# Attention with the queries on partitions: the product with V, the division and the norm by token row

## The chip, the cores and the metric

The kernel runs on one core of one Trainium2 chip. The metric is the device time of one execution in microseconds (us). A core has five engines, each with its own queue of instructions that it works through in order: TensorE (PE, matrix products and transposes, with PEld for its weight loads), VectorE (DVE), ScalarE (ACT), GpSimd (POOL) and SyncE (SP), which here issues the transfers (DMA). An engine that waits for one instruction's operands holds up all that stands behind it in its queue.

## The reference

One step of a decoder layer, for 1024 prompt tokens and 8 running sequences of 8 tokens each (64 sample tokens), width 1024:

```python
x = x + 0.5 * rms_norm(swiglu(rms_norm(x, norm_ffn1_pre), ffn1_w_gu, ffn1_w_down), norm_ffn1_post)
h = rms_norm(x, norm_mix_pre)
z = h @ w_in + b_in
q, k, v, hq, hf, hi, hg = jnp.split(z, cumsum(IN_SPLITS)[:-1], axis=-1)
a, k_new, v_new = attend(q, k, v, attn_sinks)     # 8 heads of 64, 2 kv heads, window 128
a = rms_norm(a, attn_out_norm)                    # over all 512 columns of a token
...                                               # HGRN2 on hq, hf, hi, hg gives o
mix = jnp.concatenate([a, o], axis=-1) @ w_out
x = x + rms_norm(mix, norm_mix_post)
x = x + 0.5 * rms_norm(swiglu(rms_norm(x, norm_ffn2_pre), ffn2_w_gu, ffn2_w_down), norm_ffn2_post)
```

The probabilities of a head divide by a sum that has the sink as one more term:

```python
m = jnp.maximum(jnp.max(s, axis=-1, keepdims=True), sk)
p = jnp.exp(s - m)
den = jnp.sum(p, axis=-1, keepdims=True) + jnp.exp(sk - m)
return p / den
```

For the prompt, attention works in blocks of 128 queries against 256 keys (the block before and its own).

## The kernel before

**Groups and stages.** The tokens are worked on in three groups: group 0 holds two prompt blocks of 128 and the 64 sample tokens (320 columns), groups 1 and 2 hold three prompt blocks each (384). The stages are FFN1, the mixer and FFN2. In the mixer, `w_in_units(n)` makes the projections of group n, `mixer(n)` runs attention and HGRN2 on it, `w_out_units(n)` multiplies with w_out. Every large product is three products in fp32r (`mm` L278, L279, L280: high and low parts), so a weight that arrives by DMA (`raw`, L262 or L880) is split by ACT (L255) and DVE (L256: `w`, `wspl`) before PE can use it.

**What sets the order.** PE should always have large products, and the small work goes between them. Attention blocks (`attn_block`, L1110), HGRN2 blocks (`hgrn_block`), norms and transposes are generators. `mixer(n)` runs one step of HGRN2 and one of attention in turn. Between the units of a large product `tick()` advances these streams by rates (1.0 step for mixer 1 and 1.3 for mixer 2 among them); `need(name)` finishes one that must be done. Each `yield` in a generator ends a step. So the products of FFN1 of group 1 run beside the mixer of group 0, those of `w_in_units(2)` and w_out beside the mixer of group 1, and so on. After that a scheduler orders the instructions once, when the program is built, by buffers that come free and by its own model of durations; the order on each engine is then fixed.

**Buffers.** Tiles of [128, 512] come from a ring of 8 (`t2`): the probabilities, their transposes, rows of x (`xt`), squares and outputs share it. PE writes small results to 4 PSUM banks (`ax`) and products to 4 others (`mm`). `raw` has 3 slots.

**Attention of one block.** For each of two values of pr (two heads of each of the two kv heads): scores (`sc`, L1127), mask and row maximum (L1135), exponent with row sum (L1144), the sink's exponent (L1146, L1147), sum and reciprocal (L1149, L1150), scaling of the probabilities (L1156 on ACT for g = 1, L1158 on DVE for g = 0), 8 transposes into two banks `pT` (L1165), two copies to SBUF on DVE (L1168), and the product with V. There V is stationary (64 columns for one kv head) and the transposed probabilities of two heads move:

```python
PE.matmul(ob[64 * g:64 * g + 64, pr * 256:pr * 256 + 256],
          vn[:, vb, g * 64:g * 64 + 64],
          pT[g][:, :2 * wk].rearrange("p (i k t) -> p k i t", i=2, k=nk)[:, kb], ...)
```

The result `pv` has features on partitions and tokens on columns. `finish_attn_t` (L1087) takes the norm over features: squares on ACT (L1090), four products with a column of ones (`ms`, L1094), reciprocal root on DVE (L241 to L249), a diagonal matrix (L1098), a product of ones with it (L1100) that puts the factor on all partitions, a copy (L1102) and four multiplications on DVE (L1105). `put_mix` (L1064) writes high and low parts for w_out (L1067, L1068). The sample tokens, whose result has tokens on partitions, go through `finish_attn` (L1070).

**The input of group 1 to the mixer.** This stream, "c1", runs beside the end of FFN1 and the mixer of group 0. `half_n` multiplies FFN1's result with a row of gains (`gb`, loaded at L400), `post_n` adds the input x: for three blocks and two halves a tile `xt` is loaded (L424), DVE computes `big` from it (L426), and `x1N` is stored (L427). `pre_n` takes the next norm (L394 and on), and PE transposes the result (`tr`, L454) to `h` (L458, L459), which `w_in_units(1)` multiplies.

**The bias row.** The 512 columns of the HGRN value projection have their bias on the columns: a row tile `bhi` that is loaded once at the start of the mixer and added at L1057.

## Time and profile before

| | |
|---|---|
| time, median of 3 runs | 2049.44 us (2048.64 to 2050.24) |
| span of the profiled execution | 2045.3 us |
| mean granted clock of PE | 0.988 |
| profiled execution's own time | not listed apart; the median is 4.1 us above the span |
| DVE, ACT, POOL busy | 71%, 46%, 27% of the span |

The span runs from the first to the last instruction. A granted clock below 1 means that PE worked at a lower rate for part of the time. The slices of part 2 of the page show how busy each engine is in each fortieth of the span (51 us each); the digits are tenths:

```profile
PE   9999999999999999899999998999999999999998
DVE  5776667885568557777678756766889888655667
PEclk9999999999999999799999998999999999999999
```

The 7 in the third row stands at slice 17, the 8 at slice 25. The mixer lies between about 628 and 1410 us.

### The profile page before, as it was taken

Reading aid. Unit: us, or ns where it says so; the run is one execution under the profiler, and the core shown is the slowest. Engines: PE = TensorE matmul, PEld = TensorE weight load, DVE = VectorE, ACT = ScalarE, POOL = GpSimd, SP = SyncE. Lnnn points to the kernel's source line nnn. Section 1 sums busy time; section 2 is a strip of 40 time slices with the busy share of each in tenths; the row PEclk is TensorE's granted clock in tenths of the full one; section 3 lists DMA queues with packets and bytes.
Section 4 is the critical chain, followed back from the end, with each engine's and each line's share of the span. In section 5 each row is a group of like instructions: output and inputs, shape, how many; then the busy total and the mean of one; then the engine's idle time right before and its main releaser. Section 6 shows DMA issues by size and latency. Waiting matters only on the chain.

```text
span 2045.3 us, 34828 instructions
## 1 busy us (share of the span) xinstructions
PE 2006.7 (98%) x13273; PEld 1856.7 (91%) x13273; DVE 1452.6 (71%) x2493; ACT 933.5 (46%) x1679; POOL 550.1 (27%) x508
## 2 busy tenths in 40 slices
PE   9999999999999999899999998999999999999998
PEld 8999999999998987697898897878999999999886
DVE  5776667885568557777678756766889888655667
ACT  6534333444455445435344444544544444444552
POOL 0013433654113101311113310210046554510201
PEclk9999999999999999799999998999999999999999
DMA  8455445556777545556434243525565556576874
GB/s 254 140 158 169 139 156 164 200 182 219 238 235 213 159 149 171 160 145 184 127 96 138 87 141 94 163 87 184 168 193 200 191 188 209 195 241 222 289 257 136
DMA packets 372368, 360.09 MB, mean 176 GB/s; under 512 B 40590, under 2 KB 294361, under 8 KB 372185
## 3 DMA queue, kind: packets, MB, share of 16 engines
q1 hardware_dynamic: 371401, 356.42, 55.2%
q8 instruction: 104, 1.70, 0.3%
q10 hardware_dynamic: 800, 1.44, 0.2%
q14 instruction: 63, 0.52, 0.1%
HBM read 279.85 MB, written 78.94 MB: 175 GB/s over the span
## 4 chain that ended last, share of the span: by engine, by line
PE 91%; DVE 3%; DMA 3%; ACT 1%; issue 1%; SPq 0%; DVEq 0%; ACTq 0%
PE mm L278 27%; PE mm L279 26%; PE mm L280 26%; PE c L280 1%; PE c L278 1%; PE c L279 1%; PE sc L1127 1%; DMA ar<-fa 1%; PE pv L1176 1%; DMA raw<-in_ffn_w_gu_dram 1%; PE lv L1204 1%; PE pT L1165 1%; PE tr L497 1%; DVE w L256 1%; DMA xt<-in_x_prompt_dram 0%
## 5 line engine op out<-in xcount | busy, mean ns | idle before, releaser
L278 PE MATMUL mm<-h,wsph 128*128 128x320 f32 (+1 forms) x1296 | 414.7, 322 | 3.7 <-ACT sg L632 2.2
L279 PE MATMUL mm<-h,wsph 128*128 128x320 f32 (+1 forms) x1296 | 412.5, 319 | 0.0
L280 PE MATMUL mm<-h,wspl 128*128 128x320 f32 (+1 forms) x1296 | 411.7, 318 | 0.0
L255 ACT CAST wsph<-raw 128x1024 fp32r<-128x1024 f32 x202 | 211.3, 1048 | 293.9 <-PE mm L279 237.1
L256 DVE TENSOR_TENSOR wspl<-raw,wsph 128x1024 fp32r<-128x1024 f32 x202 | 251.0, 1245 | 119.3 <-ACT wsph L255 118.5
L256 DVE TENSOR_TENSOR w<-raw,w 128x512 fp32r<-128x512 f32 (+1 forms) x226 | 250.0, 1110 | 84.9 <-ACT w L255 82.8
L255 ACT CAST w<-raw 128x512 fp32r<-128x512 f32 (+1 forms) x226 | 169.6, 754 | 207.3 <-PE mm L279 109.8
L278 PEld LDWEIGHTS mm<-h,wsph 128*128 128x128 f32 x1296 | 244.6, 189 | 11.0 <-issue 3.1
L280 PEld LDWEIGHTS mm<-h,wspl 128*128 128x128 f32 x1296 | 244.7, 189 | 4.0 <-issue 3.5
L279 PEld LDWEIGHTS mm<-h,wsph 128*128 128x128 f32 x1296 | 245.0, 189 | 3.2 <-issue 2.6
L278 PE MATMUL mm<-h,w 128*128 128x384 f32 x704 | 235.8, 335 | 1.2 <-DVE big L725 1.2
L279 PE MATMUL mm<-h,w 128*128 128x384 f32 x704 | 235.8, 335 | 0.0
L280 PE MATMUL mm<-h,w 128*128 128x384 f32 x704 | 230.5, 335 | 0.0
L279 PE MATMUL mm<-w,h 128*128 128x512 f32 x462 | 181.6, 393 | 0.0
L278 PE MATMUL mm<-w,h 128*128 128x512 f32 x462 | 180.8, 395 | 0.5 <-DVE big L905 0.5
L280 PE MATMUL mm<-w,h 128*128 128x512 f32 x462 | 179.5, 392 | 0.0
L280 PE MATMUL mm<-big,w 128*128 128x384 f32 x528 | 176.8, 335 | 1.5 <-DVE w L256 1.5
L279 PE MATMUL mm<-big,w 128*128 128x384 f32 x528 | 176.7, 335 | 0.0
L278 PE MATMUL mm<-big,w 128*128 128x384 f32 x528 | 176.6, 335 | 0.0
L709 POOL TENSOR_TENSOR big<-big 128x384 f32<-128x384 f32 x88 | 111.7, 1269 | 236.5 <-ACT big L722 116.2
L256 DVE TENSOR_TENSOR w<-t,w 128x512 fp32r<-128x512 f32 x176 | 160.5, 922 | 17.5 <-ACT w L255 17.0
L278 PEld LDWEIGHTS mm<-h,w 128*128 128x128 f32 x704 | 132.2, 188 | 1.6 <-DVE big L725 1.6
(359 smaller groups left out, 3881.2 us busy)
## 6 DMA issues: line engine op xcount, KB each, us to landing
raw<-in_ffn_w_gu_dram SPq DMA_DIRECT2D x156, 512.0 KB
raw<-in_ffn_w_down_dram SPq DMA_DIRECT2D x74, 512.0 KB
raw<-in_w_in_dram SPq DMA_DIRECT2D x54, 512.0 KB
ar<-fa SPq DMA_DIRECT2D x70, 384.0 KB
big<-in_ffn_w_down_dram SPq DMA_DIRECT2D x88, 256.0 KB
fb<-big SPq DMA_DIRECT2D x44, 512.0 KB
raw<-fb SPq DMA_DIRECT2D x40, 512.0 KB
fa<-big SPq DMA_DIRECT2D x22, 768.0 KB
```

Of the source, the lines that this page charges most:

```text
L255: S.copy(hi, src)
L256: (lo_eng or V).tensor_tensor(lo, src, hi.bitcast(F32), op=ALU.subtract)
L278: PE.matmul(out, a[0], b[0], start=first, stop=False, skip_group_check=resume)
L279: PE.matmul(out, a[0], b[1], start=False, stop=False, skip_group_check=resume)
L280: PE.matmul(out, a[1], b[0], start=False, stop=last, skip_group_check=resume)
L497: PE.transpose(bank[:, i * P:(i + 1) * P], y[kh][:, i, k * P:(k + 1) * P], ident)
L709: G.tensor_tensor(e[:, i], e[:, i], e[:, i + 1], op=ALU.mult)
L1127: PE.matmul(banks[g][:, i * 256:i * 256 + wk], zq[64 * g:64 * g + 64, 2 * pr + i, b * P:(b + 1) * P], kx[64 * g:64 * g + 64, k0:k0 + wk], ...
L1165: PE.transpose(bank[:, (i * nk + kb) * P:(i * nk + kb + 1) * P], pt[g][:, i, kb * P:(kb + 1) * P], ident)
L1176: PE.matmul(ob[64 * g:64 * g + 64, pr * 256:pr * 256 + 256], vn[:, vb, g * 64:g * 64 + 64], pT[g][:, :2 * wk].rearrange("p (i k t) -> p k ...
L1204: PE.matmul(b4[cs, a, :32], x[:, a, cs], y[:, a, cs], start=True, stop=True)
```

## The change

For the prompt blocks the roles in the product with V are swapped: the transposed probabilities (128 x 128) are stationary, and the 64 columns of V move. Its result has tokens on partitions and 512 features on columns. The probabilities are not divided before they are transposed. After both values of pr the sink's exponent, the sums and the reciprocals are taken once for 8 heads, and one multiplication of 128 x 512 divides the result. The norm is `finish_attn`, as for the sample tokens: square with a row sum on ACT, one multiplication with the row's factor and the norm weights, which lie as a row tile (`aon`), four transposes (`oT`), and `put_mix` straight from PSUM. `finish_attn_t` is gone. The copy of the second `pT` bank moves from DVE to ACT. `aon` takes the place of `bhi` in its pool; `bhi` is loaded in each `w_in_units` into a tile of the ring of 8. An attention block has 11 steps instead of 10, the samples' finish 3 instead of 2. Lines behind the removed ones have smaller numbers: L426 is now L422, L256 is L252, L278 to L280 are L274 to L276.

```diff
--- before.py
+++ after.py
@@ -158,10 +158,6 @@
         put(C_HGN, A["hg_out_norm"], 1)
-        for half in range(2):
-            nc.sync.dma_start(rows[C_AON:C_AON + 4, half * 64:half * 64 + 64],
-                              A["attn_out_norm"][0:1, half * 256:half * 256 + 256].rearrange(
-                                  "o (m d) -> (o m) d", d=64))
         bank = axbank()
...
@@ -972,8 +968,11 @@
         def t2(shape=(P, 512)):
             return tmp2("t2", shape)
 
-        bhi = tp.tile([P, 512], F32, tag="bhi", name="bhi")
-        nc.sync.dma_start(bhi, A["b_in"][0:1, 1792:2304].partition_broadcast(P))
+        aon = tp.tile([P, 512], F32, tag="aon", name="aon")
+        for half in range(2):
+            nc.sync.dma_start(aon.rearrange("p (m g d) -> p g m d", m=4, g=2)[:, half],
+                              A["attn_out_norm"][0:1, half * 256:half * 256 + 256].partition_broadcast(P).rearrange(
+                                  "p o (m d) -> p (o m) d", d=64))
 
...
@@ -1045,6 +1044,8 @@
             S.activation(z["hq"][:, :, :w], z["hq"][:, :, :w], AF.Silu)
             hv = z["v"] = big(F32, (P, 3, 512))
+            bhi = tmp2("bhi")
+            nc.sync.dma_start(bhi, A["b_in"][0:1, 1792:2304].partition_broadcast(P))
             banks = [mmbank() for _ in range(nb)]
...
@@ -1073,38 +1074,13 @@
             S.activation(junk[:r], o[:r], AF.Square, accum_out=sm[:r, 0, 0:1])
             V.tensor_scalar(sm[:r, 0, 0:1], sm[:r, 0, 0:1], 1.0 / 512, EPS, op0=ALU.mult, op1=ALU.add)
             rsqrt(sm[:r, 1, 0:1], sm[:r, 0, 0:1], (sm[:r, 2, 0:1], sm[:r, 3, 0:1]))
-            V.tensor_scalar(o[:r], o[:r], sm[:r, 1, 0:1], None, op0=ALU.mult)
+            V.scalar_tensor_tensor(o[:r], o[:r], sm[:r, 1, 0:1], aon[:r], op0=ALU.mult, op1=ALU.mult)
+            yield
             yield
             b4 = axbank("oT").rearrange("p (c t) -> p c t", c=4)
             for c in range(4):
                 PE.transpose(b4[:, c, :r], o[:r, c * P:(c + 1) * P], ident[:r, :r])
-            m = t2((P, 4, P))
-            V.tensor_tensor(m[:, :, :r], b4[:, :, :r],
-                            cols[:, C_AON:C_AON + 4].unsqueeze(2).to_broadcast([P, 4, r]), op=ALU.mult)
-            put_mix(n, 0, sl, m[:, :, :r])
-            yield
-
-        def finish_attn_t(n, ob, sl):
-
-            sm, sq = small(), t2()
-            S.activation(sq, ob, AF.Square)
-            yield
-            bank = axbank("ms")
-            for m in range(4):
-                PE.matmul(bank[:, P:P + 1], sq[:, m * P:(m + 1) * P], ones[:, 0:1], start=m == 0, stop=m == 3)
-            V.tensor_scalar(sm[:, 0, 0:1], bank[:, P:P + 1], 1.0 / 512, EPS, op0=ALU.mult, op1=ALU.add)
-            rsqrt(sm[:, 1, 0:1], sm[:, 0, 0:1], (sm[:, 2, 0:1], sm[:, 3, 0:1]))
-            dg = sq[:, :P]
-            V.tensor_scalar(dg, ident, sm[:, 1, 0:1], None, op0=ALU.mult)
-            yield
-            PE.matmul(bank[:, :P], ones, dg, start=True, stop=True)
-            rb = sq[:, P:2 * P]
-            S.copy(rb, bank[:, :P])
-            o = t2((P, 4, P))
-            for m in range(4):
-                V.scalar_tensor_tensor(o[:, m], ob[:, m * P:(m + 1) * P], cols[:, C_AON + m:C_AON + m + 1], rb,
-                                       op0=ALU.mult, op1=ALU.mult)
-            put_mix(n, 0, sl, o)
+            put_mix(n, 0, sl, b4[:, :, :r])
             yield
 
         def attn_block(n, b):
@@ -1143,19 +1119,7 @@
                         hd = 4 * g + 2 * pr + i
                         S.activation(pt[g][:, i, :wk], pt[g][:, i, :wk], AF.Exp, bias=sm[:, 1, hd:hd + 1],
                                      scale=0.125, accum_out=mx[:, 1, hd:hd + 1])
-                V.tensor_tensor(of(sm[:, 2], pr), of(sinkb, pr), of(sm[:, 0], pr), op=ALU.subtract)
-                S.activation(of(sm[:, 2], pr), of(sm[:, 2], pr), AF.Exp)
                 yield
-                V.tensor_tensor(of(mx[:, 2], pr), of(mx[:, 1], pr), of(sm[:, 2], pr), op=ALU.add)
-                V.reciprocal(of(mx[:, 3], pr), of(mx[:, 2], pr))
-                for g in range(2):
-                    for i in range(2):
-                        hd = 4 * g + 2 * pr + i
-                        t, r_ = pt[g][:, i, :wk], mx[:, 3, hd:hd + 1]
-                        if g:
-                            S.activation(t, t, AF.Copy, scale=r_)
-                        else:
-                            V.tensor_scalar(t, t, r_, None, op0=ALU.mult)
                 yield
                 pT = []
                 for g in range(2):
@@ -1165,21 +1129,31 @@
                             PE.transpose(bank[:, (i * nk + kb) * P:(i * nk + kb + 1) * P],
                                          pt[g][:, i, kb * P:(kb + 1) * P], ident)
                     t = t2()
-                    V.tensor_copy(t[:, :2 * wk], bank[:, :2 * wk])
+                    (S.copy if g else V.tensor_copy)(t[:, :2 * wk], bank[:, :2 * wk])
                     pT.append(t)
                 yield
                 if ob is None:
                     ob = axbank("pv")
-                for kb in range(nk):
-                    vb = b + kb + (1 if first else 0)
+                for i in range(2):
                     for g in range(2):
-                        PE.matmul(ob[64 * g:64 * g + 64, pr * 256:pr * 256 + 256],
-                                  vn[:, vb, g * 64:g * 64 + 64],
-                                  pT[g][:, :2 * wk].rearrange("p (i k t) -> p k i t", i=2, k=nk)[:, kb],
-                                  start=kb == 0, stop=kb == nk - 1, skip_group_check=True)
+                        c = (2 * pr + i) * P + 64 * g
+                        for kb in range(nk):
+                            vb = b + kb + (1 if first else 0)
+                            PE.matmul(ob[:, c:c + 64], pT[g][:, (i * nk + kb) * P:(i * nk + kb + 1) * P],
+                                      vn[:, vb, g * 64:g * 64 + 64], start=kb == 0, stop=kb == nk - 1)
                 if pr == 0:
                     yield
-            yield from finish_attn_t(n, ob, slice(b * P, (b + 1) * P))
+            V.tensor_tensor(sm[:, 2], sinkb, sm[:, 0], op=ALU.subtract)
+            S.activation(sm[:, 2], sm[:, 2], AF.Exp)
+            V.tensor_tensor(mx[:, 2], mx[:, 1], sm[:, 2], op=ALU.add)
+            V.reciprocal(mx[:, 3], mx[:, 2])
+            yield
+            o = t2()
+            V.tensor_tensor(o.rearrange("p (m g d) -> p m g d", m=4, g=2),
+                            ob.rearrange("p (m g d) -> p m g d", m=4, g=2),
+                            mx[:, 3].rearrange("p (g m) -> p m g", g=2).unsqueeze(3).to_broadcast([P, 4, 2, 64]),
+                            op=ALU.mult)
+            yield from finish_attn(n, o, P, slice(b * P, (b + 1) * P))
 
         def intra(n, c0, r, top, last_q, res):
```

The order that the scheduler makes of it differs over all of the mixer. Three places follow; in a row stand the line, the operation, what it writes and reads, and its shape.

The first is SP's queue at the start of group 1's input. `gb` is the row of gains, `xt` a tile of x, `x1N` the store of a sum, `raw` from `fb` a weight of FFN1's last product (kept in DRAM), `raw` from `in_w_in` one of `w_in_units(1)`. Before:

```order
L400 DMA gb_7894<-in_norm_ffn_post_dram 128x512
L880 DMA raw_8444<-fb_115 128x512
L424 DMA xt_8092<-in_x_prompt_dram 128x512
L424 DMA xt_8096<-in_x_prompt_dram 128x512
L262 DMA raw_8661<-in_w_in_dram 128x8x128
L427 DMA x1N_96<-big_5759 128x512
L427 DMA x1N_96<-big_6059 128x512
L262 DMA raw_8715<-in_w_in_dram 128x8x128
L262 DMA raw_8783<-in_w_in_dram 128x8x64 x2
L424 DMA xt_8120<-in_x_prompt_dram 128x512
L424 DMA xt_8124<-in_x_prompt_dram 128x512
L424 DMA xt_8177<-in_x_prompt_dram 128x512
```

Now:

```order
L876 DMA raw_8359<-fb_115 128x2x512
L420 DMA xt_8066<-in_x_prompt_dram 128x512
L420 DMA xt_8070<-in_x_prompt_dram 128x512
L420 DMA xt_8083<-in_x_prompt_dram 128x512
L876 DMA raw_8409<-fb_115 128x512
L423 DMA x1N_96<-big_5757 128x512
L420 DMA xt_8087<-in_x_prompt_dram 128x512
L258 DMA raw_8594<-in_w_in_dram 128x8x128
L423 DMA x1N_96<-big_6057 128x512
L423 DMA x1N_96<-big_5757 128x512
L423 DMA x1N_96<-big_6057 128x512
L420 DMA xt_8152<-in_x_prompt_dram 128x512
```

Two of the six tiles of x stood ahead of the first w_in load, and three such entries ahead of the third tile; now four stand ahead of the first of them, and the last two behind three stores of x1N. The load of `gb` now stands three rows ahead of what is shown.

The second is DVE at the same place. `w` is a split weight of FFN1's last product, `wspl` one of `w_in_units(1)`, `big` with `xt` the sum of group 1's input, `cm` and `t` belong to HGRN2, `sm` to the norms and sums. Before, from the last two splits of that product on, with eight rows of masks (L1135) and three more of attention left out at "...", as in the rows of now:

```order
L426 SCALAR_TENSOR_TENSOR big_6059<-big_6059,sm_7144,xt_8096 128x512
L256 TENSOR_TENSOR w_8394<-raw_8391,w_8393 128x1024
L256 TENSOR_TENSOR w_8447<-raw_8444,w_8446 128x512
L1223 COPY_PREDICATED cm_7933<-lm_88,lv_8059 128x128
L1239 TENSOR_TENSOR t_1112_7926<-t_1112_7926,t_1114_7928 128x128x2
...
L426 SCALAR_TENSOR_TENSOR big_5759<-big_5759,sm_7144,xt_8120 128x512
L256 TENSOR_TENSOR wspl_8664<-raw_8661,wsph_8663 128x1024
L426 SCALAR_TENSOR_TENSOR big_6059<-big_6059,sm_7144,xt_8124 128x512
L426 SCALAR_TENSOR_TENSOR big_5759<-big_5759,sm_7144,xt_8177 128x512
L1223 COPY_PREDICATED cm_7933<-lm_87,lv_8151 128x128
L1239 TENSOR_TENSOR t_1112_7926<-t_1112_7926,t_1114_7928 128x64x4
L1149 TENSOR_TENSOR sm_7823<-sm_7823,sm_7822 128x2x2
```

Now:

```order
L422 SCALAR_TENSOR_TENSOR big_5757<-big_5757,sm_7145,xt_8066 128x512
L252 TENSOR_TENSOR w_8312<-raw_8309,w_8311 128x1024
L422 SCALAR_TENSOR_TENSOR big_6057<-big_6057,sm_7145,xt_8070 128x512
L422 SCALAR_TENSOR_TENSOR big_5757<-big_5757,sm_7145,xt_8083 128x512
L422 SCALAR_TENSOR_TENSOR big_6057<-big_6057,sm_7145,xt_8087 128x512
L1197 COPY_PREDICATED cm_7912<-lm_87,lv_8114 128x128
L1213 TENSOR_TENSOR t_1112_7905<-t_1112_7905,t_1114_7907 128x64x4
...
L422 SCALAR_TENSOR_TENSOR big_5757<-big_5757,sm_7145,xt_8152 128x512
L252 TENSOR_TENSOR w_8362<-raw_8359,w_8361 128x1024
L422 SCALAR_TENSOR_TENSOR big_6057<-big_6057,sm_7145,xt_8156 128x512
L1197 COPY_PREDICATED cm_7912<-lm_86,lv_8192 128x128
L1213 TENSOR_TENSOR t_1112_7905<-t_1112_7905,t_1114_7907 128x32x8
```

Before, four of the six sums stood behind the last split `w`; now all six stand ahead of the last one (it follows two rows behind what is shown last, after L1148 and L1149), and one ahead of each of the two before it.

The third is PE, where the products of FFN1's last matrix pass into those of group 1's mixer. `mm` are the products, `lv` and `l` belong to HGRN2, `tr` are the transposes of group 1's input. Before:

```order
L280 MATMUL mm_8274<-w_8393,h_8450 128x512
L1204 MATMUL lv_8217<-t_1112_7926,t_1113_7927 32x32 x16
L1165 MATMUL pT_8257<-ident,t_1139_8106 128x128 x4
L1165 MATMUL pT_8264<-ident,t_1140_8109 128x128 x4
L1204 MATMUL lv_8304<-t_1112_7926,t_1113_7927 32x32 x16
L1176 MATMUL pv_8024<-t_1159_8262,vn_6438 64x256
L1176 MATMUL pv_8024<-t_1161_8269,vn_6438 64x256
L1176 MATMUL pv_8024<-t_1159_8262,vn_6438 64x256
L1176 MATMUL pv_8024<-t_1161_8269,vn_6438 64x256
L1228 MATMUL l_1180_8370<-t_1112_7926,t_1113_7927 32x32 x8
L1094 MATMUL ms_8420<-ones,t_1173_8333 128x1 x4
L1228 MATMUL l_1187_8435<-t_1112_7926,t_1113_7927 64x64 x4
```

Now:

```order
L275 MATMUL mm_8234<-w_8362,h_8415 128x512
L1202 MATMUL l_1178_8338<-t_1112_7905,t_1113_7906 32x32 x8
L1142 MATMUL pv_8074<-vn_6437,t_1169_8294 128x64 x2
L1142 MATMUL pv_8074<-vn_6437,t_1171_8301 128x64 x2
L1142 MATMUL pv_8074<-vn_6437,t_1169_8294 128x64 x2
L1142 MATMUL pv_8074<-vn_6437,t_1171_8301 128x64 x2
L276 MATMUL mm_8234<-w_8361,h_8415 128x512
L274 MATMUL mm_8235<-w_8361,h_8415 128x512
L275 MATMUL mm_8235<-w_8362,h_8415 128x512
L276 MATMUL mm_8235<-w_8361,h_8415 128x512
L274 MATMUL mm_8235<-w_8361,h_8415 128x512
L275 MATMUL mm_8235<-w_8362,h_8415 128x512
```

Before, eleven rows follow each other without a product between them, from `lv` to the second `l`; now the `pT` of this pair stand among products further ahead, `ms` is gone, and products stand between `pv` and the next `l`.

6 lines of the change are left out of this document (3 added, 3 removed).

## Prediction

> **What bounds the kernel now.** I read the page first, then the table by windows, the waits of the matrix engine (PE), and the timelines of the windows in which PE loses time.
>
> ```profile
> PE 2006.7 (98%) x13273; PEld 1856.7 (91%) x13273; DVE 1452.6 (71%) x2493; ACT 933.5 (46%) x1679; POOL 550.1 (27%) x508
> ```
> ```profile
> PE 91%; DVE 3%; DMA 3%; ACT 1%; issue 1%; SPq 0%; DVEq 0%; ACTq 0%
> ```
> ```profile
> core 0: 2045.3 us, clock 0.988
> ```
>
> The first line is part 1 of the page (busy us, share, instructions), the second the chain that ended last, the third the span and the mean granted clock. PE is busy for 2006.7 of 2045.3 us and holds 91% of the chain that ended last. So the time is PE's work, plus the places where PE waits, plus what the granted clock takes there. The windows show those places (columns: window, length, busy us and instructions of PE, PE's weight loads, DVE, ACT, POOL, then PE clock, DMA share, GB/s):
>
> ```profile
> 844.00:872.00 28.00, 19.66 (x154) 14.67 (x153) 20.22 (x56) 13.82 (x30) 4.90 (x8) 0.63 0.50 131
> 872.00:1237.00 365.00, 364.96 (x3008) 319.40 (x3006) 264.93 (x637) 162.07 (x328) 76.91 (x104) 1.00 0.46 132
> 1237.00:1275.00 38.00, 32.65 (x208) 26.92 (x209) 25.86 (x89) 14.84 (x42) 3.65 (x8) 0.87 0.33 97
> 1338.00:1364.00 26.00, 21.48 (x241) 17.49 (x240) 17.12 (x37) 13.71 (x23) 5.90 (x10) 0.87 0.32 95
> ```
>
> In the second row PE has no gap in 365 us, although attention runs there too: what DVE and ACT do there costs nothing. In the other three PE idles, and the clock falls with it. I price such a window at its idle time plus busy time x (1 - clock): 844 to 872 costs 8.3 + 19.66 x 0.37 = **15.6 us**; 1237 to 1275 costs 5.4 + 32.65 x 0.13 = **9.6 us**; 1338 to 1364 costs 4.5 + 2.8 = **7.3 us**. Together 32.5 us, the most that a change of waits in these three can return.
>
> PE's waits, with their sum, number and longest, say who is late there:
>
> ```profile
> PE pT L1165 <- DVE t L1158: 4.4, 2, 2.5
> ...
> PE kT L1277 <- DVE h L459: 1.9, 1, 1.9
> PE lv L1204 <- DVE sm L247: 1.7, 1, 1.7
> PE l L1228 <- DVE t L1239: 1.5, 1, 1.5
> ...
> PE lv L1204 <- DVE sm L1149: 1.5, 1, 1.5
> ...
> PE sc L1127 <- DVE st L1295: 1.3, 1, 1.3
> ...
> PE pv L1176 <- DVE t L1168: 1.1, 1, 1.1
> ```
>
> Three of these releasers (L1158, L1149, L1168) are DVE steps of attention which the change removes or halves. "sm L1149" and "sm L247" before lv are only what DVE last did: it is one queue in order, and lv waits for the step behind. So the question in each window is what DVE was doing.
>
> **The change part by part.** First PE's own work, since a microsecond there is a microsecond of the kernel. Before, each pass over a pair of heads issues 8 pv instructions (an fp32 product is two). From the timeline of PE (start, busy, line, count):
>
> ```profile
> 1230.34 1.08 PE L1176 MATMUL pv<-t,vn 128*64 128x256 f32 x8
> 1231.35 0.50 PE L279 MATMUL mm<-wspl,h 128*128 128x512 f32 x1
> ...
> 1254.97 0.65 PE L1176 MATMUL pv<-t,vn 128*64 128x256 f32 x2
> 1255.55 0.33 PE L1277 MATMUL kT<-ident,t 128*128 128x128 f32 x1
> ...
> 1260.28 0.95 PE L1094 MATMUL ms<-ones,t 128*128 128x1 f32 x8
> 1261.09 0.47 PE L1283 MATMUL av<-big,At 128*128 128x128 f32 x2
> ```
> ```profile
> 1125.47 1.05 PE L1290 MATMUL u<-big,t 128*128 128x128 f32 x8
> 1126.27 0.48 PE L278 MATMUL mm<-wsph,h 128*128 128x512 f32 x1
> ```
>
> From start to next start, eight pv take 1.01 us in one piece; a group that is broken in 2 + 6 takes 0.58 + 1.01. There are 15 groups (x120 in all), and 9 of the pairs were broken: 15 x 1.01 + 9 x 0.58 = 20.4 us. Afterwards there are 240 instructions with 128 stationary and 64 moving columns. No row has that shape. The nearest has the same 128 stationary columns and one moving column: eight ms in 0.81 us, 0.101 each; eight u (128 moving) take 0.80 as well, so the moving width between 1 and 128 does not matter. 240 x 0.101 = 24.3 us, up to 26.7 with 0.08 us more at the entry of each half group (30); I take 25.5, so **+5.1 us**. Ends: had no group been broken, before would be 15.1 and the difference up to +11.6; had before cost the 24.8 us that its group shows as busy, the difference would be as little as -0.5.
>
> The Trainium skill ("TensorE: Matmul & The Clock Gate", section "Back-to-back issue gap") gives about 25 ns for a matmul of at most 64 moving columns taken alone; by it 240 would cost 6 us, and the sum would be about 19 us lower. The same page's "LDWEIGHTS (loading the stationary operand)" has the load at columns / 1.2 ns, 107 ns for 128 whatever the moving width, 25.6 us for 240. The trace speaks for the second: one moving column costs 101 ns, as many as 128 do.
>
> Gone from PE are the 64 ms (8 x 0.81 = -6.5 us) and the 16 L1100 that spread the factor over the partitions; new are four transposes per block:
>
> ```profile
> 869.99 0.38 PE L1100 MATMUL ms<-t,ones 128*128 128x128 f32 x2
> 870.39 0.45 PE L278 MATMUL mm<-h,wsph 128*128 128x384 f32 x1
> ...
> 1339.58 0.60 PE L1259 MATMUL hT<-ident,t 128*128 128x128 f32 x4
> 1340.11 0.65 PE L1176 MATMUL pv<-t,vn 128*64 128x256 f32 x2
> ```
>
> A pair of L1100 takes 0.40, x 8 blocks = -3.2 us at most; four transposes take 0.53, x 8 = +4.2. **PE's own work: 5.1 - 6.5 - 3.2 + 4.2 = -0.4 us**, bounds -6 to +7. So the change neither wins nor loses on PE's work; it must come from the waits.
>
> DVE gets lighter exactly in these stages (line, shapes, count, busy us and mean ns, idle before):
>
> ```profile
> L1168 DVE COPY t<-pT 128x512 f32<-128x512 f32 x28 | 18.6, 682 | 3.3 <-PE pT L1165 3.2 <-POOL big L359 0.2
> L426 DVE SCALAR_TENSOR_TENSOR big<-big,sm,xt 128x512 f32<-128x512 f32 x18 | 14.7, 835 | 9.6 <-DMA xt<-in_x_prompt_dram 8.2 <-DMA xt<-x1N 1.3
> L1158 DVE TENSOR_SCALAR t<-t,sm 128x256 f32<-128x256 f32 x28 | 10.0, 400 | 0.4
> L1105 DVE SCALAR_TENSOR_TENSOR t<-pv,cols,t 128x128 f32<-128x128 f32 x32 | 9.0, 343 | 3.2 <-ACT t L1102 3.2
> L1255 DVE TENSOR_TENSOR t<-av,sm 128x512 f32<-128x512 f32 x8 | 5.5, 689 | 0.2
> ```
>
> Away: half of L1168 (-9.3), L1158 (-10.0), L1105 (-9.0). New: one division of 128x512 per block (8 x 0.689 by L1255 = +5.5) and one step with factor and weights (8 x 0.835 by L426 = +6.7). Net about -16 us of DVE. ACT loses its half of the scaling and gains the second copy of pT, which hides on an engine that is 46% busy; four more activation table loads appear, 1.283 us each by this row, 5.1 us in all, and cost the path only where ACT releases PE (estimate 0 to 3 us, inside the new waits below):
>
> ```profile
> L1144 ACT ACT_TABLE_LOAD x7 | 9.0, 1283 | 1.2 <-DVE sm L1146 1.1
> ```
>
> **844 to 872.** What is late there is group 1's input to the mixer, which needs the rows of x (xt):
>
> ```profile
> 821.71 0.33 SPq L880 DMA_DIRECT2D raw<-fb  x1
> 822.13 5.11 SPq L424 DMA_DIRECT2D xt<-in_x_prompt_dram  x2
> 829.15 0.38 SPq L262 DMA_DIRECT2D raw<-in_w_in_dram  x1
> ...
> 834.55 2.16 SPq L262 DMA_DIRECT2D raw<-in_w_in_dram  x3
> 836.80 2.86 SPq L424 DMA_DIRECT2D xt<-in_x_prompt_dram  x3
> ```
> ```profile
> 842.40 0.75 DVE L426 SCALAR_TENSOR_TENSOR big<-big,sm,xt 128x512 f32<-128x512 f32 x1 [4.35 <-DMA xt<-in_x_prompt_dram]
> ```
>
> The third xt is issued at 836.8, behind four loads of w_in that wait for raw buffers, and DVE stands 4.35 us for it at 842.4; behind it in DVE's queue are L1149 and L1158 of attention and the weight splits, so PE gets neither pT nor new weights. In the new order (shown with the change) four xt stand ahead of the first w_in load, not two, and all six L422 stand among the last splits of the FFN. The third xt then comes where the second did, at about 827 instead of 836.8: 8 to 10 us earlier, as long as the whole idle of this window. What is late next is the fifth xt, behind three x1N stores; and its L422 now stands ahead of a split that PE needs. I take **-10 of 15.6 us**; ends -14 and +8.5 (the slower rival).
>
> **1237 to 1275.** Here lv, sc, lv and l, and later u, ms, sc, L1100, sc follow one another with no product between them. In the new order the u stands alone among products and sc has moved away from it; L1100 and its bank are gone. I take **-5 of 9.6 us**, ends -9 and +1.
>
> **1338 to 1364.** L1158 in front of pT (2.5 us, the longest wait) is gone, but pT and pv still stand close together: **-2 of 7.3 us**, ends -6 and +3.
>
> **New waits.** The bias row bhi, loaded once before, is loaded three times; for group 1 it stands in SP's queue directly behind the 15 reads of osc:
>
> ```profile
> 954.29 5.13 SPq L1372 DMA_DIRECT2D t<-osc  x15
> ```
>
> The adds L1058 wait for it, and behind them on DVE are the evictions that free PE's banks. Issue of the reads 5.1 us and a landing of some 3 us against a distance of about 9 us of products: 0 to 6 us. With the sample steps now close to one another and ACT's tables: **+3**, ends 0 and +8.
>
> **Sum.** -0.4 - 10 - 5 - 2 + 3 = -14.4 us on the span of 2045.3 gives 2030.9. The median of the runs, 2049.44, lies 4.1 us above the span; the run of the profile is not listed apart. So **2035 us**.
>
> **The rivals.** (A) The stalls move: xt comes earlier but the splits behind it come later, and DVE's lighter load goes into idle time, as in the window of 365 us where DVE's work costs nothing. Then only the 1338 part (-2) remains: 2047. For it: DVE idles 29% already. Against: three waits name steps that vanish. (B) Slower: the fifth xt lands as late as the third did (842.4). Then the split behind it, needed at about 840, comes some 4 us late and the last one too; PE idles about 12 us instead of 8.3, with the remaining products of that matrix (4.1 us) and the 19.7 us at 0.63 or less: 12 + 23.8 x 0.5 = 24 against 15.6, +8.5. With -5 - 2 + 3 and PE's -0.4 that is +4 and 2054. It decides when the fifth xt lands after about 838. Against it: t2 buffers come free earlier. (C) All three windows close: -32.5 + 3 - 0.4 is -29.9, so 2019. Against it: at 1338 PE's order still has pT next to pv. (E) The price of pv follows the moving columns: by the first pv row 0.126 us for 256 columns, so 0.032 for 64 and 7.6 us for 240, 17.9 less than I took: 2017. Against it: ms with one column costs 0.101. This is what the first of the two sections named above comes to. That the steps would still be there can be left out: they are gone from the instruction lists.
>
> **How the numbers follow.** Forecast (2024 to 2043) 0.48; A 0.22; B 0.15; C 0.12; E 0.03. The range may leave out 0.2: its lower end, 2018, is just under C and cuts E and half of C's spread, its upper end, 2055, half of B's. A measurement of this kernel tells about 0.2% (4.1 us) from no change: faster is the forecast, C, E and a sixth of A, 0.67; same is most of A and a little of B, 0.18; slower 0.15.
>
> **What would show it.** Right: the window before the first tr of group 1 shows a clock above 0.9 and no wait of DVE above 2 us for xt; PE's pv groups take 1.6 to 1.8 us per 16; total PE busy within 25 us below 2006.7, the fall being half-clock time. Wrong: pv near 0.5 us per 16 (E), a wait of mm for a split in front of group 1's mixer (B), hv adds waiting for bhi by more than 4 us, or three windows of clock below 0.9 at other places (A).

## The result, and the profile after

| | before | after |
|---|---|---|
| time, median | 2049.6 us (2048.64 to 2050.24) | 2029.24 us (2027.45 to 2030.84) |
| span of the profiled execution | 2045.3 us | 2027.8 us |
| mean granted clock | 0.988 | 0.990 |

The ratio is 0.9902, 95% interval 0.9888 to 0.9916: 20 us faster. The forecast was 2035 us, with a range of 2018 to 2055. The span fell by less, 17.5 us: the profiled execution of the changed kernel took 2029.57 us, 1.8 us above its span, so that of the kernel before took about 2047, some 2.5 us below its median.

The page of the changed kernel, part 1 (busy us, share of the span, instructions):

```profile
PE 1995.8 (98%) x13345; PEld 1865.0 (92%) x13345; DVE 1431.3 (71%) x2396; ACT 931.9 (46%) x1659; POOL 544.5 (27%) x508
```

The kernel is still bound by PE, at the same 98%. PE is busy for 10.9 us less and idle for 6.6 us less. The windows say where (window, length, busy us and instructions of PE, PEld, DVE, ACT, POOL, then PE clock, DMA share, GB/s). The first answers to 844 to 872 of before, the third to 1237 to 1275, the last to 1338 to 1364. The first score products of mixer 2 stand at 1194.6 us before and at 1203.3 now, so the last three lie within mixer 2 (the expectations further down say mixer 2's start for its second block):

```profile
830.00:860.00 30.00, 27.35 (x228) 22.56 (x229) 24.71 (x71) 19.30 (x50) 4.35 (x9) 1.00 0.67 174
...
940.00:980.00 40.00, 33.93 (x218) 24.53 (x217) 21.29 (x49) 9.91 (x18) 8.13 (x7) 0.79 0.38 105
...
1220.00:1260.00 40.00, 39.58 (x349) 34.63 (x348) 26.46 (x79) 15.40 (x39) 5.75 (x10) 1.00 0.36 105
1260.00:1300.00 40.00, 36.58 (x375) 31.26 (x373) 26.90 (x70) 24.00 (x49) 9.27 (x16) 0.83 0.50 159
1300.00:1370.00 70.00, 69.70 (x679) 63.83 (x678) 48.73 (x123) 37.12 (x78) 12.56 (x21) 1.00 0.34 99
```

Priced as before (idle time plus busy time x (1 - clock)):

| place | before | after |
|---|---|---|
| end of FFN1, group 1's input (844 / 830) | 15.6 | 2.7 |
| end of the samples' mixer (in 872 to 1237 / 940) | 0 | 6.1 + 33.93 x 0.21 = 13.2 |
| mixer 2, from its first block to its second (1237 / 1220) | 9.6 | 0.4 |
| mixer 2, second block (1275 to 1338 / 1260) | 0 | 3.4 + 36.58 x 0.17 = 9.6 |
| mixer 2, third block (1338 / 1300) | 7.3 | 0.3 |
| sum | 32.5 | 26.2 |

All three old windows are nearly closed, and two new ones have opened. Together the five give only 6.3 of the 17.5 us by which the span fell. The price takes the mean clock of a window for all of its busy time; counted instruction by instruction, the five give 7.6 us. Gaps elsewhere give 0.9. PE's waits name the new windows (line waited for, us in total, times, longest):

```profile
PE mm L274 <- DVE big L1058: 4.0, 1, 4.0
PE lv L1178 <- DVE t L1213: 2.2, 2, 1.4
```

The first is the wait for the bias row bhi at 966 us, the second stands at 1275 to 1280.

**The other half is PE's own work.** I summed, for each line, the time from a PE instruction's start to the next one's start, at most to its own end, at half weight where the clock was halved. The sum fell from 1989.1 to 1980.1 us, by 8.9 us:

| line | before | after | difference | predicted |
|---|---|---|---|---|
| pv (L1176, now L1142) | 20.9 | 27.1 | +6.1 | +5.1 |
| ms (L1094) | 6.8 | 0 | -6.8 | -6.5 |
| spreading (L1100) | 2.3 | 0 | -2.3 | -3.2 |
| oT (L1080, now L1082) | 0.4 | 3.5 | +3.1 | +4.2 |
| sc (L1127, now L1103) | 23.8 | 19.2 | **-4.6** | not named |
| products mm (L278 to L280) | 1807.8 | 1805.2 | -2.6 | not named |
| samples' su, sav | 12.5 | 10.3 | -2.2 | not named |
| all others | | | +0.4 | |

The samples' lines ran partly at half clock afterwards, where the half weight may take off too much.

The four terms of the forecast add up to +0.1, as forecast (-0.4). What was not seen is the fall of the score products, whose number and shapes did not change. The groups in the stretch of the mixer, first of the kernel before, then of the changed one (count, busy us, mean ns):

```profile
L1127 PE MATMUL sc<-kx,big 64*128 64x256 f32 x112 | 25.0, 413 | 1.7 <-DVE st L1295 1.3 <-ACT t L1102 0.4
```
```profile
L1103 PE MATMUL sc<-kx,big 64*128 64x256 f32 x112 | 21.1, 421 | 0.0
```

In time order the reason shows. Before, with one pair's group in two pieces:

```profile
1079.06 1.13 PE L1127 MATMUL sc<-kx,big 64*128 64x256 f32 x4
1080.12 0.44 PE L280 MATMUL mm<-h,wspl 128*128 128x384 f32 x1
...
1083.62 1.13 PE L1127 MATMUL sc<-kx,big 64*128 64x256 f32 x4
1084.68 0.46 PE L1204 MATMUL lv<-t,t 128*32 128x32 f32 x32
```

After, in one:

```profile
1075.73 1.13 PE L1103 MATMUL sc<-kx,big 64*128 64x256 f32 x8
1076.80 0.44 PE L275 MATMUL mm<-h,wsph 128*128 128x384 f32 x1
```

Four instructions take 1.06 us, and eight take 1.07: a group that is broken costs PE one microsecond more. The pieces of four hold one kv head each, the group of eight both, so the two heads' products overlap only when they are issued together. Of 16 groups 9 were whole before, 13 after. Why the order breaks a group is shown at one place only: at 1265 and 1267 us of the kernel before, the two pieces wait for L1295 on DVE (1.29 us) and for the copy L1102 on ACT (0.41 us), which read two of the four small PSUM banks. At the others PE waits for nothing that the profile shows; that they too were broken for want of a bank is likely, but not shown.

For pv, the price that no row had shown (start, busy, line, count):

```profile
844.81 2.00 PE L1142 MATMUL pv<-vn,t 128*128 128x64 f32 x16
846.62 0.48 PE L276 MATMUL mm<-w,h 128*128 128x512 f32 x1
...
1242.37 1.89 PE L1142 MATMUL pv<-vn,t 128*128 128x64 f32 x16
1244.07 0.48 PE L275 MATMUL mm<-wspl,h 128*128 128x512 f32 x1
```

1.81 and 1.70 us for 16, 0.106 to 0.113 each: the price of 128 stationary columns, whether 1, 64 or 128 columns move. The Trainium skill ("TensorE: Matmul & The Clock Gate", section "LDWEIGHTS (loading the stationary operand)") gives 107 ns for 128 columns by its formula, which the trace bears out; the 25 ns that its section "Back-to-back issue gap" has for a product alone of up to 64 moving columns is not what this stream of loads and products pays.

**Group 1's input.** SP's queue after (start, us, line, count):

```profile
817.33 1.43 SPq L420 DMA_DIRECT2D xt<-in_x_prompt_dram  x3
...
824.32 0.38 SPq L420 DMA_DIRECT2D xt<-in_x_prompt_dram  x1
826.11 0.38 SPq L258 DMA_DIRECT2D raw<-in_w_in_dram  x1
827.18 1.64 SPq L423 DMA_DIRECT2D x1N<-big  x3
828.92 1.64 SPq L420 DMA_DIRECT2D xt<-in_x_prompt_dram  x2
```

The third tile of x is issued before 819, not at 836.8, and the fifth at 828.9. DVE waits for it, as forecast, with a split of weights behind it:

```profile
834.18 0.75 DVE L422 SCALAR_TENSOR_TENSOR big<-big,sm,xt 128x512 f32<-128x512 f32 x1 [2.89 <-DMA xt<-in_x_prompt_dram]
834.85 1.22 DVE L252 TENSOR_TENSOR w<-raw,w 128x1024 fp32r<-128x1024 f32 x1
```

The sum over it starts at 834, ahead of the 838 from which the slower rival would have decided. PE loses 0.9 us there.

### The profile page after: what moved, and what is told of

Read it like the earlier page. It is cut to its first block, busy times and chain, and to the rows that moved or that the text cites. A ratio compares the mean times of both kernels' runs of the same rounds, so it can differ in the third digit from the quotient of the medians.

```text
span 2027.8 us, 34845 instructions
## 1 busy us (share of the span) xinstructions
PE 1995.8 (98%) x13345; PEld 1865.0 (92%) x13345; DVE 1431.3 (71%) x2396; ACT 931.9 (46%) x1659; POOL 544.5 (27%) x508
## 4 chain that ended last, share of the span: by engine, by line
PE 91%; DVE 3%; DMA 3%; issue 1%; ACT 1%; SPq 0%; POOL 0%; DVEq 0%; ACTq 0%; POOLq 0%
PE mm L274 27%; PE mm L276 27%; PE mm L275 27%; PE c L276 1%; PE c L274 1%; PE c L275 1%; PE pv L1142 1%; PE sc L1103 1%; DMA raw<-in_ffn_w_gu_dram 1%; PE lv L1178 1%; DVE w L252 1%; DMA xt<-in_x_prompt_dram 1%; PE pT L1129 1%; PE tr L493 1%; DVE wspl L252 0%
## 5 line engine op out<-in xcount | busy, mean ns | idle before, releaser
L274 PE MATMUL mm<-h,wsph 128*128 128x320 f32 (+1 forms) x1296 | 413.4, 321 | 4.6 <-DVE big L1058 4.0
L276 PE MATMUL mm<-h,wspl 128*128 128x320 f32 (+1 forms) x1296 | 411.2, 318 | 0.2 <-DVE wspl L252 0.2
L252 DVE TENSOR_TENSOR wspl<-raw,wsph 128x1024 fp32r<-128x1024 f32 x202 | 253.6, 1257 | 109.8 <-ACT wsph L251 108.0
L252 DVE TENSOR_TENSOR w<-raw,w 128x512 fp32r<-128x512 f32 (+1 forms) x226 | 246.5, 1095 | 88.9 <-ACT w L251 87.0
L274 PEld LDWEIGHTS mm<-h,wsph 128*128 128x128 f32 x1296 | 244.5, 189 | 8.9 <-DVE big L1058 4.5
L276 PEld LDWEIGHTS mm<-h,wspl 128*128 128x128 f32 x1296 | 244.8, 189 | 2.6 <-issue 1.7
L274 PE MATMUL mm<-h,w 128*128 128x384 f32 x704 | 235.6, 335 | 1.8 <-DVE big L721 1.8
L276 PE MATMUL mm<-h,w 128*128 128x384 f32 x704 | 230.3, 335 | 0.0
L274 PE MATMUL mm<-w,h 128*128 128x512 f32 x462 | 180.2, 393 | 0.0
L276 PE MATMUL mm<-w,h 128*128 128x512 f32 x462 | 180.0, 392 | 0.0
L276 PE MATMUL mm<-big,w 128*128 128x384 f32 x528 | 176.6, 335 | 1.0 <-DVE w L252 1.0
L274 PE MATMUL mm<-big,w 128*128 128x384 f32 x528 | 176.6, 334 | 0.1
L252 DVE TENSOR_TENSOR w<-t,w 128x512 fp32r<-128x512 f32 x176 | 162.1, 930 | 15.3 <-ACT w L251 15.0
L274 PEld LDWEIGHTS mm<-h,w 128*128 128x128 f32 x704 | 132.1, 188 | 2.2 <-DVE big L721 2.1
```

The lines of the kernel that those rows point to most:

```text
L252: (lo_eng or V).tensor_tensor(lo, src, hi.bitcast(F32), op=ALU.subtract)
L274: PE.matmul(out, a[0], b[0], start=first, stop=False, skip_group_check=resume)
L276: PE.matmul(out, a[1], b[0], start=False, stop=last, skip_group_check=resume)
```

## The experiments

Each ratio is to the kernel before, run on the same chip; the changed kernel has 0.9902 (0.9888 to 0.9916). A thousandth is 2 us. Where the intervals of two ratios overlap, as those of runs 1, 2, 7 and 8 do with that of the changed kernel, the traces must tell what differs.

**1. The bias row on ACT's queue.** Changed kernel with

```diff
-            nc.sync.dma_start(bhi, A["b_in"][0:1, 1792:2304].partition_broadcast(P))
+            nc.scalar.dma_start(bhi, A["b_in"][0:1, 1792:2304].partition_broadcast(P))
```

> The changed kernel, with the three loads of the bias row bhi issued by ACT's queue instead of SP's, so that the one of group 1 no longer stands behind the 15 reads of osc. Theory: PE's 4.0 us wait at 966 us is this load (issued at 966.4, landed 3.3 us later), and the clock is halved because of it: the wait goes, the halved stretch of 17 us shrinks to 7 or less, and the kernel takes 2019 to 2024 us. Rival: the clock falls at 958.6, before that wait, because the sample steps of attention and HGRN2 follow one another there without products: the wait of 4 us goes but the halved stretch stays 14 us or longer, 2024 to 2027 us.

Measured: 2024.29 us, ratio 0.9886 (0.9873 to 0.99), at the border between theory and rival; the span is 5.7 us shorter. First the changed kernel's chain at this place (start, us, what), then that of the experiment:

```profile
960.84 0.34 SPq L1341
961.24 0.32 SPq L1346
...
966.06 0.30 SPq L1346
966.41 3.30 DMA bhi<-in_b_in_dram
969.73 0.70 DVE big L1058
970.48 0.69 PE mm L274
```
```profile
960.43 0.41 PE spv L1337 x8
960.87 3.33 DMA bhi<-in_b_in_dram
964.22 0.70 DVE big L1058
964.97 0.69 PE mm L274
```

In the changed kernel 15 reads of osc (L1346) are issued one by one, 0.34 us each, with bhi behind them. In the experiment bhi is issued 5.5 us earlier and PE's wait of 4.04 us shrinks to 0.59. The halved stretch is 10.2 us long, not 17.1. That length lies between theory (7 or less) and rival (14 or more): the wait is the load's, but the clock fell at 957.9 here and at 958.6 in the changed kernel, ahead of the wait in both. So part of the window belongs to the samples' steps standing close to one another. Even on ACT's queue the load starts only when spv has run: it had no free tile before that, or ACT stood behind one.

**2. The bias row one projection earlier.** Changed kernel with the two lines of bhi ahead of `z["hq"] = big()`.

> The changed kernel, with bhi loaded on SP one projection earlier (ahead of the four products of hq), so that its row stands ahead of the osc reads; the tile holds one of the ring of 8 for longer. Theory: the same gain as with ACT's queue, 2019 to 2025 us, since only the load's place matters. Rival: the order of the whole mixer is made anew by the longer hold, and new waits of DVE for free tiles give back 5 us or more: 2027 to 2035 us.

Measured: 2030.62 us, ratio 0.9918 (0.9904 to 0.9931), no measurable difference from the changed kernel. The rival's time came, but not by its cause. The wait for bhi is 1.9 us, and a new one stands 10 us later:

```profile
PE oT L1082 <- DVE t L1077: 7.4, 1, 7.4
```
```profile
974.48 4.79 SPq L1346 DMA_DIRECT2D t<-osc  x14
```

L1077 is the last step of the samples' norm, which waits for the same reads of osc, and oT now stands directly behind the samples' products. The reads are what is late; the order decides who waits for them.

**3. The division in its old place.** Changed kernel in which the probabilities are scaled ahead of their transposes, and the product is copied:

```diff
+                        if g:
+                            S.activation(t, t, AF.Copy, scale=r_)
+                        else:
+                            V.tensor_scalar(t, t, r_, None, op0=ALU.mult)
...
-            V.tensor_tensor(o.rearrange("p (m g d) -> p m g d", m=4, g=2), ...
+            V.tensor_copy(o, ob)
```

> The changed kernel with the old place of the division: probabilities are scaled by 1/sum before their transposes (DVE for g = 0, ACT for g = 1, sink exponent per pair), and the product's result is only copied. The new product and the new norm stay. Theory: what closed the windows at 844 and 1237 is the lighter DVE queue and the shorter way from scores to transposes, so these come back in part and the kernel takes 2034 to 2042 us. Rival: it is the norm and the product (no ms, no diagonal, fewer banks and tiles held) that closed them, and the kernel takes 2026 to 2032 us.

Measured: 2036.06 us, ratio 0.9947 (0.9932 to 0.9961): 7 to 9 us slower than the changed kernel. The theory's time held, its places only in part:

```profile
830.00:860.00 30.00, 25.71 (x217) 22.07 (x216) 24.53 (x69) 18.33 (x51) 4.30 (x9) 0.94 0.69 185
940.00:985.00 45.00, 36.41 (x228) 27.40 (x228) 23.88 (x57) 10.41 (x21) 8.34 (x8) 0.77 0.40 109
1220.00:1260.00 40.00, 39.58 (x363) 33.22 (x362) 23.59 (x59) 17.70 (x45) 6.66 (x11) 1.00 0.36 106
1260.00:1300.00 40.00, 35.55 (x355) 31.99 (x354) 31.48 (x100) 25.84 (x55) 7.49 (x11) 0.83 0.54 171
```

By price: 5.8 at the end of FFN1 (2.7 in the changed kernel, 15.6 before), 17.0 at the samples (13.2), 0.4 at the change from mixer 2's first block to its second (0.4), 10.5 in its second block (9.6). So the rest of the change, without the later division, takes 9.8 of the 15.6 us of the first window away and closes the one of 1237 wholly. The later division is worth 3 us in the first window and 4 at the samples; another 2 to 3 us lie at 1108, where the clock is halved for 3.4 us in this run.

**4. The bias row's reload alone.** The kernel before, with bhi in the ring, loaded in each `w_in_units`.

> The kernel before, with one part of the change alone: bhi loaded in each w_in_units into a tile of the ring of 8. Theory: this part alone costs, since the load of group 1 stands behind osc reads there too: a wait of mm for the add of bhi of 2 to 6 us and 2052 to 2060 us. Rival: the cover of 9 us or more is enough in the old order and nothing changes beyond the order's own scatter: 2046 to 2052 us.

Measured: 2048.38 us, ratio 1.0003 (0.9994 to 1.0011): nothing, the rival. The same load that costs PE a wait of 4 us in the changed order is covered in the old one, where PE is not idle at all between 940 and 1000.

**5. Group 1's input earlier, attention as before.** The kernel before, with

```diff
-    RA0, RA1, RB0, RB1 = 1.2, 0.75, 0.6, 0.8
+    RA0, RA1, RB0, RB1 = 1.2, 0.9, 0.6, 0.8
```

> The kernel before, with one number changed: the rate of group 1's input stream is 0.9 steps per tick, not 0.75. By its order four tiles of x then stand ahead of the first w_in load, as in the changed kernel, and four of the six sums ahead of the last two splits; attention is as before. Theory: the place of these loads alone makes the window at 844 us: its loss falls from 15.6 to 5 us or less, and the kernel takes 2036 to 2042 us. Rival: the long way through attention on DVE (scaling, two copies, norm) makes it: the loss stays above 10 us and the kernel takes 2045 to 2052 us.

Measured: 2047.76 us, ratio 1.0 (0.999 to 1.0009). The theory's time and loss did not come, the rival's did. But the run does not set all six tiles of x where the changed kernel has them. Four come early; the last two stand behind four loads of w_in in SP's queue, as the third did before. Window, SP, PE and DVE of this run:

```profile
830.00:870.00 40.00, 29.12 (x273) 22.46 (x272) 29.80 (x84) 20.93 (x49) 8.04 (x10) 0.79 0.47 131
```
```profile
834.43 2.35 SPq L262 DMA_DIRECT2D raw<-in_w_in_dram  x3
836.83 2.17 SPq L424 DMA_DIRECT2D xt<-in_x_prompt_dram  x2
```
```profile
845.64 1.54 PE L1165 MATMUL pT<-ident,t 128*128 128x128 f32 x6 [6.77 <-DVE t L1158]
```
```profile
842.04 0.75 DVE L426 SCALAR_TENSOR_TENSOR big<-big,sm,xt 128x512 f32<-128x512 f32 x1 [2.64 <-DMA xt<-in_x_prompt_dram]
...
845.24 0.61 DVE L1158 TENSOR_SCALAR t<-t,sm 128x256 f32<-128x256 f32 x2
```

The price is 10.9 + 29.12 x 0.21 = 17.0 us. DVE waits for the fifth tile of x and, for 0.77 us more, for the sixth, and the scaling L1158 stands behind both: PE's transposes wait 6.77 us for it. In the changed kernel DVE waits for the same fifth tile for as long (2.89 us), but with two differences: no scaling stands behind it, and the tile is issued 7.9 us earlier (828.9, not 836.83), so that DVE goes on at 834.2, not at 842.0. The run cannot tell which of the two counts. It does bring the condition of the slower rival B, the fifth tile as late as the third was before, and there the loss is 17.0 us, not the 24 named for it.

**6. The second copy on ACT alone.** The kernel before, with

```diff
-                    V.tensor_copy(t[:, :2 * wk], bank[:, :2 * wk])
+                    (S.copy if g else V.tensor_copy)(t[:, :2 * wk], bank[:, :2 * wk])
```

> The kernel before, with one part of the change alone: the copy of the second pT bank on ACT instead of DVE. Theory that DVE's load in the mixer is what counts: 9 us less of DVE work and pv no longer broken in 2 + 6 gives 5 us on PE and 5 to 10 us of the windows: 2034 to 2042 us. Rival, the order's places count: pv is broken less often (up to 5 us), the windows stay: 2043 to 2049 us.

Measured: 2037.9 us, ratio 0.9953 (0.9938 to 0.9968): 10 us faster, the theory's time. But the window at the end of FFN1 stays at 13.8 us (6.9 idle, 33.14 x 0.21), and PE's own work fell by 1.5 us only, though pv is broken three times, not nine. The largest piece, 5 us, comes from 1300 to 1410.

**7. Both copies on DVE.** The changed kernel with that line undone.

> The changed kernel with both copies of pT on DVE, as before the change. Theory: the second copy on ACT matters little in the changed kernel, since its pv takes the same time whether broken or not, DVE has room: 2026 to 2032 us. Rival: pv waits for the second copy at the tight places (mixer starts) and the windows open again: 2034 to 2040 us.

Measured: 2025.43 us, ratio 0.9895 (0.988 to 0.991): just below the theory's range, and no measurable difference from the changed kernel. The theory held, the windows did not open again. A part that is worth 10 us in the old order is worth nothing in the new one.

**8. Score products bank by bank.** The changed kernel with the two loops around the score products exchanged:

```diff
-                for i in range(2):
-                    for g in range(2):
+                for g in range(2):
+                    for i in range(2):
```

> The changed kernel with the four score products of a pair issued bank by bank (two of one kv head, then two of the other) instead of in turn, the same work in another order. Theory: score products of the two kv heads (rows 0 to 63 and 64 to 127 of the array) run side by side only when they are issued in turn; bank by bank a group of 8 takes 2 x 1.058 instead of 1.064 us, so 12 more groups cost 1.05 us each on PE, 2039 to 2045 us. Rival: a group of 8 takes the same time in either order and the earlier broken groups only waited for a bank: 2027 to 2031 us.

Measured: 2022.23 us, ratio 0.9878 (0.9863 to 0.9892). Both miss: PE takes the same time for a group in either order, so the theory fell, and the kernel is faster than the rival said: 7 us below the changed kernel by the medians, 5 by the ratios.

```profile
1076.28 1.14 PE L1103 MATMUL sc<-kx,big 64*128 64x256 f32 x8
1077.36 0.44 PE L275 MATMUL mm<-h,wsph 128*128 128x384 f32 x1
```

What counts is that all eight stand together, not their turn. The gain is the window of mixer 2's second block:

```profile
1260.00:1300.00 40.00, 37.57 (x445) 33.11 (x444) 30.21 (x77) 28.79 (x59) 12.29 (x18) 1.00 0.57 182
```

2.4 us against 9.6. There no group of sc is broken around pv any more, and the clock stays whole.

**9. The old norm's PE pieces put back.** The changed kernel with, per block, a square on ACT, the four products ms, one product that spreads, and a copy; nothing uses their result.

```diff
+            sq = t2()
+            S.activation(sq, o, AF.Square)
+            bank = axbank("ms")
+            for m in range(4):
+                PE.matmul(bank[:, P:P + 1], sq[:, m * P:(m + 1) * P], ones[:, 0:1], start=m == 0, stop=m == 3)
+            PE.matmul(bank[:, :P], ones, ident, start=True, stop=True)
+            S.copy(sq[:, P:2 * P], bank[:, :P])
```

> The changed kernel with the PE pieces of the old norm put back beside the new one, their result unused: per prompt block a square on ACT into a tile of the ring, four products of 128x1 with ones, one product that spreads over the partitions, and a copy on ACT, in one step. Theory: these pieces cost what their rows showed (6.8 and 2.3 us on PE) and the bank and the tile that they hold do no harm: 2036 to 2040 us. Rival: a bank and a tile held for so long break up score products and delay the tiles of x, and the windows open again: 2043 to 2052 us.

Measured: 2035.25 us, ratio 0.9939 (0.9924 to 0.9953), just below the theory's range. One block's pieces:

```profile
1254.37 0.94 PE L1160 MATMUL ms<-ones,t 128*128 128x1 f32 x8
1255.17 0.47 PE L1161 MATMUL ms<-ident,ones 128*128 128x128 f32 x2
1255.48 0.39 PE L1265 MATMUL av<-big,At 128*128 128x128 f32 x2
```

1.11 us, 8.8 for eight blocks; PE's own work rose by 6.0 us in sum, as other lines fell. The window at the end of FFN1 stays closed (1.6 us), and 14 of 16 score groups are whole. The samples' window grew from 13.2 to 16.1 us. So these pieces cost what their instructions cost, and a bank and a tile that are held within one step do not open the first window. The run does not put back the old norm's steps on DVE, nor the longer time for which `ms` and `pv` held their banks.

**10. The order's scatter.** The kernel before, with the exchange of run 8.

> The kernel before, with only the score products issued bank by bank, the same work. It shows how much the order alone moves the time of the kernel before. Theory: order scatter of some 5 us either way and no lasting gain, 2043 to 2054 us. Rival: bank by bank helps by itself, since the mask of one kv head can begin two products earlier, and the kernel before gains the same 7 us: 2039 to 2043 us.

Measured: 2047.65 us, ratio 1.0002 (0.9993 to 1.0012), the theory: no gain. 9 of 16 groups are whole, as before, and the window at the end of FFN1 costs 15.0 us.

**11 and 12. Together.** The changed kernel with the edits of runs 8 and 1; then with that of run 7 as well.

> The changed kernel with the score products bank by bank and the bias row on ACT's queue. Theory: the two gains stand at two different places (mixer 2's start and the samples' end) and add up: 2022.2 less about 6, 2014 to 2018 us. Rival: the order made anew at one place undoes the other: 2020 to 2026 us.

> As the run before, and both copies of pT on DVE. Theory: another 2 to 4 us, as in the changed kernel, where ACT's copy stood behind table loads at the mixer's start: 2011 to 2016 us. Rival: nothing, since the gain of that edit was the order's scatter: 2014 to 2022 us.

Measured: 2018.82 us, ratio 0.986 (0.9845 to 0.9874), and 2017.84 us, ratio 0.9854 (0.9839 to 0.9869). Both beat the changed kernel and the kernel before. The first lies between its theory's 2018 and its rival's 2020. In the second the third edit adds nothing measurable, as its rival said. Of run 11:

```profile
940.00:980.00 40.00, 36.51 (x245) 28.94 (x243) 22.61 (x50) 11.08 (x19) 8.13 (x7) 0.87 0.41 117
1260.00:1300.00 40.00, 37.71 (x424) 34.09 (x423) 31.88 (x81) 29.82 (x65) 13.35 (x19) 1.00 0.56 178
```

The samples' window costs 3.5 + 36.51 x 0.13 = 8.2 us there, and mixer 2's second block 2.3.

## Why the prediction was right, and where its steps were not

**PE's own work (-0.4, measured -8.9).** The four terms were right to about a microsecond each, and pv's 16 in 1.70 to 1.81 us came within 0.01 us of the 1.6 to 1.8 named. The step missed a term: it counted only instructions that the change adds or removes. The score products, unchanged in number, gave 4.6 us because they are broken less often. Their breaks were visible in the timeline before, as pv's were, and only pv's were counted.

**844 to 872 (-10, measured -12.9).** Size and place were right, and the reason given, the lateness of the tiles of x, fits all fourteen kernels. In the table stands the moment at which DVE takes the last tile of x for which it waited more than 1 us, beside the price of the window:

| DVE goes on at | kernels | loss |
|---|---|---|
| 842.0 to 843.4 us | before; runs 4, 5, 6, 10 | 13.8 to 17.0 us |
| 838.2 us | run 3 | 5.8 us |
| 833.7 to 835.7 us | changed; runs 1, 2, 7, 8, 9, 11, 12 | 1.6 to 3.2 us |

This is a fit and no proof: no run moves all six tiles and nothing else, and attention, which shares DVE's queue, differs too. The step was loose in one point: it moved the third tile, "as long as the whole idle of this window", but what counts is the last tile that DVE waits for. Which part of the change brings it forward stays open. Run 3 gives the later division 3 us of the loss and 4 us of the tile's time. The copy on ACT alone (run 6) and the bias row's reload alone (run 4) leave the tile late, so the rest should come with the new product and norm. Run 9 excludes the norm's PE work; the time for which pv held its bank, the old norm's steps on DVE, and the order that follows from them were not isolated.

**1237 to 1275 (-5, measured -9.2) and 1338 to 1364 (-2, measured -7.0).** Both closed further than forecast. But part of it moved rather than went: mixer 2's second block, free of loss before between 1275 and 1338, costs 9.6 us. That is rival A at one place. The three things seen at this place (PE's lv for DVE, broken score groups, DVE waiting 1.2 us at a time for tiles of x from x1N) have no single releaser; run 8 shows that another order of the same work avoids it. Why it does was not isolated.

**New waits (+3, measured 13.2).** The place and the mechanism were right: bhi behind 15 reads of osc, 5.13 us of issue and 3.30 of landing, then L1058, then PE. The mis-sized term is the price: the wait of 4.0 us was within the bounds of 0 to 8, but it was priced as time alone, and the window's 13.2 lies outside them. The three old windows had been priced with their lost clock, and this one had to be too: 33.93 us of busy time at 0.79 add 7.1. Run 1 took the wait back for 5.7 us of span and left 7.0 in the window, with the samples' steps close to one another.

**The sum.** The windows gave 6.3 us where 14 were forecast, PE's own work 8.9 where 0.4 was. The forecast of the time was near because these two errors nearly cancel, and that is luck.

**The signs.** Three came as named: a clock of 1.00 in the first window, pv's price, and PE's busy time 10.9 us lower. Two did not: DVE's wait for a tile of x was 2.89 us, not below 2, and of the 10.9 us some 9 are PE's own work, not half-clock time. Of the signs of being wrong, PE's wait behind the add of bhi reached 4.0 us, right at its limit, and the clock fell below 0.9 at two other places (0.79 and 0.83), not at three.

## What to carry to other kernels

Price a new wait like an old window: idle time plus the clock that goes with it. Where small products of two row groups must overlap, count how often the order breaks their groups: each break cost a microsecond of PE here, and for most the profile shows no wait. Of several transfers that stand in front of a queue, look at the last one that it waits for; four early tiles of six were worth nothing in run 5. And take the worth of a part from the order in which it will run: the same copy on ACT was worth 10 us in one order and nothing in the other.

## What the runs showed of the hardware

The score products of 64 rows overlap between the two halves of the array when eight stand together, in either order (1.064 us in turn in the changed kernel, 1.071 bank by bank in run 8), and not when four of one half stand alone (1.058 us for each four).

Every stretch of halved clock lasted 3.4 us or a multiple of it (3.4, 6.8, 10.2, 13.7, 17.1, 20.5 us), apart from the last one, which runs over the kernel's end. It fell without a long gap: at 958.6 us in the changed kernel PE had had one gap of 0.69 us and stood in one of 0.72, in a stretch of small products; in the 3.4 us before, PE was busy for 2.3.
